# Stick-breaking attention on one core: one mask product for the two diagonal blocks of a PSUM bank, masks between a block's two products, and the shorter block first

## The chip, the cores and the metric

The kernel runs on one core of one Trainium2 chip. The metric is the device time of one execution in microseconds; of the kernel before, three executions gave 873.54, 874.85 and 875.4 us, with a median of 874.85 us. A separate execution was profiled, and every time below that is not one of these three comes from it.

## What is computed

The program is a whole decoder block for 512 tokens of width 1024: an RMS norm, one wide input projection, stick-breaking attention and an RWKV-7 branch beside each other, a merge with gates, an MLP, a gated per-layer embedding and a last norm. The change lies in the attention, whose reference for one block of 128 queries is

```python
z = jnp.einsum('bhqd,bhkd->bhqk', q[:, :, q0:kend], k[:, :, :kend]).astype(jnp.float32) * scale
mask = s_pos < t_pos
log_om = jnp.where(mask, jax.nn.log_sigmoid(-z), 0.0)
rev = lax.cumsum(log_om, axis=log_om.ndim - 1, reverse=True)
log_w = jax.nn.log_sigmoid(z) + rev - log_om
w = jnp.where(mask, jnp.exp(log_w), 0.0)
outs.append(jnp.einsum('bhqk,bhkd->bhqd', w.astype(v.dtype), v[:, :, :kend]))
```

There are 8 heads of width 64, and a key counts only for later queries, so on the diagonal block of each key block the mask is a triangle.

## The kernel before

Keys lie on partitions and queries on columns. For one head the scores are four key blocks j = 0 to 3 of 128 keys each; block j holds the queries from j\*128 on, so the blocks are 512, 384, 256 and 128 columns wide. They fill three PSUM banks (2 KB per partition, 512 columns of float32): bank 0 holds block 0, bank 2 holds block 2, and bank 1 holds block 1 in its columns 0 to 383 and block 3 in its columns 384 to 511. `BLOCKS` (L431) gives the order of the banks and of the blocks inside one: bank 2, bank 1, bank 0.

`scores` (L440) makes one head's scores. For every block it issues three products on TensorE into the bank, `ps_z`: L453, the keys `kk` against the rounded queries `qq`; L454, the same keys against the remainders `ql`; and L455, an identity `ident_b` against the triangle `caus_b` of -1e30 and 0, both in bf16, which adds the mask to the first 128 columns of the block (its diagonal). When a bank has all its products, ScalarE takes Abs, Exp and Ln of it (L458 to L460), VectorE makes the softplus `sp` (L461), and `split` (L221, L222) turns that into a high and a low part, `sph` and `spl`. After bank 1, sums of softplus over later key blocks are made too (L465 to L476: `sums`, `sums_hi`, `sums_lo`).

`attend` (L479) goes over the banks in the same order. It adds to the same PSUM bank the running sums inside a key block (L500, weights `tri`) and those of the later key blocks (L504, weights `neg`), ScalarE takes the exponential (L505), VectorE makes its high and low parts `wh` and `wl` (L506, L507), and `output` (L488, its product L492) multiplies these with the values `vv` into `ps_o`.

Eight such heads run one after another. `drive` (L279) mixes three streams by their counts of steps: `attend` of one head, `scores` of the next, and the projections of the weight units that come later. A projection step is `mm3` (L186): three products of 512 columns (L191, L192, L193). So between the pieces of the attention TensorE always has 512-column products standing in its queue. The order written so is then changed a little by a scheduler that puts what is ready first; after that each engine runs its own queue in order and waits where an operand is missing. Weights of every product are loaded anew: the trace has one LDWEIGHTS (engine PEld) for each MATMUL.

`z(zt, j, lo, n)` (L433) gives the columns of block j inside its bank.

Of the kernel before, what the change touches and what calls it, by code (L numbers as in the profile page):

```python
# [18 lines left out]
P = 128  # L19
T = 512  # L20
# [65 lines left out]
def tile_block(ctx: ExitStack, tc: tile.TileContext, xT, xt, pT, wts, lora, cols_d, gfin_d, consts_d, out, dbg=None):  # L86
    nc = tc.nc
    act, dve, pool, pe, sync = nc.scalar, nc.vector, nc.gpsimd, nc.tensor, nc.sync
# [3 lines left out]
    def r32(ap):  # L92
        return ap.bitcast(F32)
# [126 lines left out]
    def split(hi, lo, src):  # L220
        act.copy(out=hi, in_=src)  # L221
        dve.tensor_tensor(out=lo, in0=src, in1=r32(hi), op=ALU.subtract)  # L222
# [49 lines left out]
    with ExitStack() as sA:  # L272
# [43 lines left out]
        with ExitStack() as s1:  # L316
# [3 lines left out]
            def ps_z():  # L320
                return ps1.tile([P, T], F32, name="ps_z", bufs=5)
# [52 lines left out]
            ident_b, caus_b = (p1.tile([P, P], BF16, name=n, bufs=1) for n in ("ident_b", "caus_b"))  # L374
# [53 lines left out]
                    yield from product_steps(ps, w, h)  # L428
                    projected(hp, i, ps)

            BLOCKS = ((2, (2,)), (1, (1, 3)), (0, (0,)))  # L431

            def z(zt, j, lo=0, n=None):  # L433

                b = 0 if j == 0 else (2 if j == 2 else 1)
                s = ZB[j] - BANKS[b][0] + lo
                n = ZN[j] - lo if n is None else n
                return zt[b][:, s:s + n]

            def scores(hp, hh, got):  # L440

                qq, ql, kk = heads[hp][:3]
                sp = p1.tile([P, 1280], F32, name="sp")
                sph = p1.tile([P, 1280], F32R, name="sph")
                spl = p1.tile([P, 1280], F32R, name="spl")
                zt = {}
                got.update(zt=zt, sp=sp, sph=sph, spl=spl)
                for b, js in BLOCKS:
                    zt[b] = ps_z()

                    for j in js:
                        s = slice(j * P, (j + 1) * P)
                        pe.matmul(z(zt, j), kk[hh][:, s], qq[hh][:, j * P:T], start=j < 3, stop=False, skip_group_check=True)  # L453
                        pe.matmul(z(zt, j), kk[hh][:, s], ql[hh][:, j * P:T], start=False, stop=False, skip_group_check=True)  # L454
                        pe.matmul(z(zt, j, 0, P), ident_b, caus_b, start=False, stop=True, skip_group_check=True)  # L455
                    s, n = BANKS[b]
                    e = sp[:, s:s + n]
                    act.activation(out=e, in_=zt[b][:, :n], func=AF.Abs)  # L458
                    act.activation(out=e, in_=e, func=AF.Exp, scale=-1.0)
                    act.activation(out=e, in_=e, func=AF.Ln, bias=1.0)  # L460
                    dve.scalar_tensor_tensor(out=e, in0=zt[b][:, :n], scalar=0.0, in1=e, op0=ALU.max, op1=ALU.add)  # L461
                    split(sph[:, s:s + n], spl[:, s:s + n], e)
                    if b == 1:

                        sums = p1.tile([P, 512], F32, name="sums", bufs=1)  # L465
                        hi, lo = (p1.tile([P, 640], F32R, name=name) for name in ("sums_hi", "sums_lo"))
                        for to, i in ((0, 2), (256, 1)):
                            for part, d in ((sph, hi), (spl, lo)):
                                pool.tensor_copy(out=d[:, to:to + P], in_=part[:, ZB[i]:ZB[i] + P])
                        dve.tensor_tensor(out=sums[:, 0:P], in0=sp[:, ZB[2] + P:ZB[2] + 2 * P], in1=sp[:, ZB[3]:ZB[3] + P], op=ALU.add)  # L470
                        split(hi[:, P:2 * P], lo[:, P:2 * P], sums[:, 0:P])
                        for c, other in ((0, sp[:, ZB[2]:ZB[2] + P]), (P, sums[:, 0:P])):
                            dve.tensor_tensor(out=sums[:, 256 + c:384 + c], in0=sp[:, ZB[1] + P + c:ZB[1] + 2 * P + c], in1=other, op=ALU.add)
                        pool.tensor_copy(out=hi[:, 384:640], in_=sums[:, 256:512])
                        pool.tensor_tensor(out=lo[:, 384:640], in0=sums[:, 256:512], in1=r32(hi[:, 384:640]), op=ALU.subtract)
                        got["later"] = hi, lo  # L476
                    yield

            def attend(hp, hh, got):  # L479

                vv, oo = heads[hp][3:]
                sl = HALVES[hh]
                zt, sp, sph, spl = (got[n] for n in ("zt", "sp", "sph", "spl"))
                wh = p1.tile([P, 1280], F32R, name="wh")
                wl = p1.tile([P, 1280], F32R, name="wl")
                ps_o = ps1.tile([P, T], F32, name="ps_o", bufs=1)

                def output(js):  # L488

                    for j in js:  # L490
                        for part in (wh, wl):
                            pe.matmul(ps_o[:, j * P:T], vv[:, j, hh, :, :].rearrange("p a d -> p (a d)"),  # L492
                                      part[:, ZB[j]:ZB[j] + ZN[j]], start=j == 2 and part is wh, stop=j == 0 and part is wl,
                                      skip_group_check=True)

                before = ()
                for b, js in BLOCKS:
                    s, n = BANKS[b]
                    for part in (sph, spl):
                        pe.matmul(zt[b][:, :n], tri, part[:, s:s + n], start=False, stop=False, skip_group_check=True)  # L500
                    j = js[0]
                    for part, later in zip((sph, spl), got["later"]):
                        after = (later[:, 256:640], later[:, 0:256], part[:, ZB[3]:ZB[3] + P])[j]
                        pe.matmul(z(zt, j, P), neg, after, start=False, stop=part is spl, skip_group_check=True)  # L504
                    state["exp"] = act.activation(out=sp[:, s:s + n], in_=zt[b][:, :n], func=AF.Exp)  # L505
                    dve.tensor_copy(out=wh[:, s:s + n], in_=sp[:, s:s + n])  # L506
                    dve.tensor_tensor(out=wl[:, s:s + n], in0=sp[:, s:s + n], in1=r32(wh[:, s:s + n]), op=ALU.subtract)  # L507
                    yield
                    output(before)
                    before = js  # L510
                yield
                output(before)
                act.copy(out=oo[sl], in_=ps_o[64:128])
                dve.tensor_tensor(out=oo[sl], in0=ps_o[0:64], in1=oo[sl], op=ALU.add)
                if hh == 1:
                    sync.dma_start(out=o_sb[:, hp, :], in_=oo)
# [43 lines left out]
            ahead = with_late(early())  # L560
            NSTEP = 11
            drive((3, scores(*heads_[0], parts[heads_[0]])), (NSTEP, islice(ahead, NSTEP)))
            for n, g in enumerate(heads_):
                todo = [(5, attend(*g, parts[g])), (NSTEP, islice(ahead, NSTEP))]
                if n + 1 < len(heads_):
                    todo.insert(1, (3, scores(*heads_[n + 1], parts[heads_[n + 1]])))
                drive(*todo)
# [4 lines left out]
        with ExitStack() as s2:  # L572
# [37 lines left out]
            for hp in range(HP):  # L610
                csl = slice(hp * P, (hp + 1) * P)
                for i, (name, got) in enumerate((("w0", cum_), ("a0", a_all))):
# [3 lines left out]
                    t = p2.tile([P, T], F32, name=name, bufs=HP)  # L616
# [492 lines left out]
    def kept(tt):  # L1109
        t = p4.tile([P, 512], F32, name="pl", tag="rk", bufs=4)  # L1110
        return t

    for half in range(2):
        for tt in (half * 2, half * 2 + 1):
            t = kept(tt)
# [250 lines left out]
```

## Time and profile before

| | |
|---|---|
| profiled execution, device time | 874.59 us |
| its span in the trace | 872.8 us (1.79 us lie around it) |
| three executions without profile | 873.54, 874.85, 875.4 us |
| TensorE (PE) busy | 853.0 us, 98% |
| weight loads (PEld) busy | 687.9 us, 79% |
| VectorE (DVE) busy | 676.7 us, 78% |
| ScalarE (ACT) busy | 449.3 us, 51% |
| GpSimd (POOL) busy | 78.7 us, 9% |
| mean granted clock of TensorE | 0.995 |
| the scores and masks (L453 to L455) | from 31.4 to 125.9 us of the span |

Products on TensorE overlap, and their ends are modelled in the profile, so the busy time says little of how long a product holds the engine. What does is the distance from the start of one to the start of the next; a stretch of starts that begins and ends at products of the same kind gives the time that the products in it took.

### The profile page before, as it was taken

Reading aid. Unit: us, or ns where it says so; the run is one execution under the profiler, and the core shown is the slowest. Engines: PE = TensorE matmul, PEld = TensorE weight load, DVE = VectorE, ACT = ScalarE, POOL = GpSimd, SP = SyncE. Lnnn points to the kernel's source line nnn. Section 1 sums busy time; section 2 is a strip of 40 time slices with the busy share of each in tenths; the row PEclk is TensorE's granted clock in tenths of the full one; section 3 lists DMA queues with packets and bytes.
Section 4 is the critical chain, followed back from the end, with each engine's and each line's share of the span. In section 5 each row is a group of like instructions: output and inputs, shape, how many; then the busy total and the mean of one; then the engine's idle time right before and its main releaser. Section 6 shows DMA issues by size and latency. Waiting matters only on the chain.

```text
span 872.8 us, 13418 instructions
## 1 busy us (share of the span) xinstructions
PE 853.0 (98%) x5182; PEld 687.9 (79%) x5182; DVE 676.7 (78%) x1230; ACT 449.3 (51%) x706; POOL 78.7 (9%) x136
## 2 busy tenths in 40 slices
PE   9999999999999999998999999999999999999995
PEld 6778787877777777776888888888888888888885
DVE  7899987896979888666834789858985987697666
ACT  7888887735345253524524465344434533453743
POOL 1432421003202021010000000000000000000000
PEclk9999999999999999999999999999999999999998
DMA  7212113131221225357735621531252044200422
GB/s 269 97 62 72 62 61 103 54 101 47 73 74 61 86 75 176 102 174 266 272 97 170 240 73 34 186 119 49 87 178 97 25 141 149 97 1 0 171 71 97
DMA packets 32272, 95.32 MB, mean 109 GB/s; under 512 B 3664, under 2 KB 3664, under 8 KB 32208
## 3 DMA queue, kind: packets, MB, share of 16 engines
q1 hardware_dynamic: 32208, 94.46, 32.4%
q8 instruction: 41, 0.67, 0.3%
q14 instruction: 23, 0.19, 0.1%
HBM read 83.96 MB, written 10.49 MB: 108 GB/s over the span
## 4 chain that ended last, share of the span: by engine, by line
PE 74%; DVE 13%; ACT 7%; DMA 3%; issue 2%; SPq 0%; ACTq 0%; DVEq 0%
PE ps_m L191 13%; PE ps_m L193 13%; PE ps_m L192 13%; PE ps_m L208 7%; PE ps_m L206 7%; PE ps_m L207 7%; DVE w_lo L176 2%; DMA w_raw<-in_wts_dram 1%; ACT hx L1039 1%; PE ps_o L492 1%; PE ps_g L898 1%; DVE LX L836 1%; PE ps_z L500 1%; PE ps_s L936 1%; PE ps_c L927 1%
## 5 line engine op out<-in xcount | busy, mean ns | idle before, releaser
L175 ACT CAST w_hi<-w_raw 128x1024 fp32r<-128x1024 f32 x94 | 99.0, 1053 | 175.6 <-PE ps_m L192 114.8
L176 DVE TENSOR_TENSOR w_lo<-w_raw,w_hi 128x1024 fp32r<-128x1024 f32 x94 | 115.2, 1225 | 38.2 <-ACT w_hi L175 37.7
L191 PE MATMUL ps_m<-h_hi,w_hi 128*128 128x512 f32 x320 | 130.7, 410 | 0.0
L192 PE MATMUL ps_m<-h_lo,w_hi 128*128 128x512 f32 x320 | 128.9, 403 | 0.0
L193 PE MATMUL ps_m<-h_hi,w_lo 128*128 128x512 f32 x320 | 127.6, 399 | 0.0
L191 PE MATMUL ps_m<-hx,w_hi 128*128 128x512 f32 x256 | 99.7, 390 | 0.4 <-ACT hx L1039 0.4
L192 PE MATMUL ps_m<-hx,w_hi 128*128 128x512 f32 x256 | 99.6, 390 | 0.0
L193 PE MATMUL ps_m<-hx,w_lo 128*128 128x512 f32 x256 | 99.5, 389 | 0.0
L193 PEld LDWEIGHTS ps_m<-h_hi,w_lo 128*128 128x128 f32 x320 | 60.3, 188 | 11.7
L192 PEld LDWEIGHTS ps_m<-h_lo,w_hi 128*128 128x128 f32 x320 | 60.5, 189 | 11.3 <-DVE h_lo L349 1.1
L191 PEld LDWEIGHTS ps_m<-h_hi,w_hi 128*128 128x128 f32 x320 | 60.7, 190 | 10.5 <-ACT h_hi L348 0.4
L191 PEld LDWEIGHTS ps_m<-hx,w_hi 128*128 128x128 f32 x256 | 48.0, 188 | 10.4 <-ACT hx L1039 0.6
L192 PEld LDWEIGHTS ps_m<-hx,w_hi 128*128 128x128 f32 x256 | 48.1, 188 | 10.2 <-DVE hx L1040 0.2
L193 PEld LDWEIGHTS ps_m<-hx,w_lo 128*128 128x128 f32 x256 | 48.1, 188 | 9.9
L206 PE MATMUL ps_m<-w_hi,fS 128*128 128x512 f32 x128 | 49.8, 389 | 0.0
L207 PE MATMUL ps_m<-w_lo,fS 128*128 128x512 f32 x128 | 49.8, 389 | 0.0
L208 PE MATMUL ps_m<-w_hi,fS 128*128 128x512 f32 x128 | 49.8, 389 | 0.0
L208 PE MATMUL ps_m<-w_hi,fA 128*128 128x512 f32 x96 | 37.3, 389 | 0.0
L206 PE MATMUL ps_m<-w_hi,fA 128*128 128x512 f32 x96 | 37.3, 389 | 0.0
L207 PE MATMUL ps_m<-w_lo,fA 128*128 128x512 f32 x96 | 37.3, 389 | 0.0
L221 ACT CAST fS<-sums 128x256 fp32r<-128x256 f32 (+1 forms) x32 | 19.9, 620 | 33.3 <-DVE sums L1131 33.3
L1204 DVE TENSOR_TENSOR xs<-ps_m,xs 128x512 f32<-128x512 f32 x56 | 35.8, 681 | 0.0
(378 smaller groups left out, 1876.0 us busy)
## 6 DMA issues: line engine op xcount, KB each, us to landing
w_raw<-in_wts_dram SPq DMA_DIRECT2D x98, 512.0 KB, 3.4
gates<-gg SPq DMA_DIRECT2D x16, 256.0 KB, 2.0
x_in<-in_xT_dram SPq DMA_DIRECT2D x8, 256.0 KB, 5.1
tmp<-gates SPq DMA_DIRECT2D x8, 256.0 KB, 4.2
upsb<-tmp SPq DMA_DIRECT2D x8, 256.0 KB, 2.8
ga<-upsb SPq DMA_DIRECT2D x8, 256.0 KB, 6.3
gb<-gates SPq DMA_DIRECT2D x8, 256.0 KB, 5.8
xs<-in_xt_dram SPq DMA_DIRECT2D x4, 512.0 KB, 7.8
```

The costliest lines, as they stand in the source:

```text
L175: act.copy(out=hi, in_=raw)
L176: dve.tensor_tensor(out=lo, in0=raw, in1=r32(hi), op=ALU.subtract)
L191: pe.matmul(ps, wh, xh[:, k, t], start=first, stop=False)
L192: pe.matmul(ps, wh, xl[:, k, t], start=False, stop=False)
L193: pe.matmul(ps, wl, xh[:, k, t], start=False, stop=last)
L206: pe.matmul(ps, xh[:, k + j], wh, start=first and j == 0, stop=False, skip_group_check=True)
L207: pe.matmul(ps, xh[:, k + j], wl, start=False, stop=False, skip_group_check=True)
L208: pe.matmul(ps, xl[:, k + j], wh, start=False, stop=last and j == 1, skip_group_check=True)
L221: act.copy(out=hi, in_=src)
L492: pe.matmul(ps_o[:, j * P:T], vv[:, j, hh, :, :].rearrange("p a d -> p (a d)"), part[:, ZB[j]:ZB[j] + ZN[j]], start=j == 2 and part is wh, ...
L500: pe.matmul(zt[b][:, :n], tri, part[:, s:s + n], start=False, stop=False, skip_group_check=True)
L1204: dve.tensor_tensor(out=xb, in0=pss[t2], in1=xb, op=ALU.add)
```

## The change

```diff
-            BLOCKS = ((2, (2,)), (1, (1, 3)), (0, (0,)))
+            BLOCKS = ((2, (2,)), (1, (3, 1)), (0, (0,)))
...
-                    for j in js:
+                    n = len(js)
+                    diagonal = zt[b].rearrange("p (q t) -> p q t", t=P)[:, 0::3, :] if n == 2 else z(zt, js[0], 0, P)
+                    mask = caus_b.rearrange("p (o t) -> p o t", o=1).broadcast_to([P, n, P]) if n == 2 else caus_b
+                    for i, j in enumerate(js):
                         s = slice(j * P, (j + 1) * P)
-                        pe.matmul(z(zt, j), kk[hh][:, s], qq[hh][:, j * P:T], start=j < 3, stop=False, skip_group_check=True)
-                        pe.matmul(z(zt, j), kk[hh][:, s], ql[hh][:, j * P:T], start=False, stop=False, skip_group_check=True)
-                        pe.matmul(z(zt, j, 0, P), ident_b, caus_b, start=False, stop=True, skip_group_check=True)
+                        pe.matmul(z(zt, j), kk[hh][:, s], qq[hh][:, j * P:T], start=i == 0, stop=False, skip_group_check=True)
+                        if i == n - 1:
+                            pe.matmul(diagonal, ident_b, mask, start=False, stop=False, skip_group_check=True)
+                        pe.matmul(z(zt, j), kk[hh][:, s], ql[hh][:, j * P:T], start=False, stop=True, skip_group_check=True)
...
-                    j = js[0]
+                    j = js[-1]
```

In bank 1 the two blocks change places, so the 128-column block 3 comes first, in `scores` and in `output`. Their two masks become one product of 256 columns: it reads the triangle twice and writes two runs of 128 columns, the first and the last quarter of the bank. And the mask of every bank now stands between the last block's product with `qq` and its product with `ql`, where it stood behind both. Per head there are 11 products in place of 12, and 88 in place of 96 in all.

On TensorE bank 1 of a head in the steady stretch (the third head, the products before it are the last of `attend` for the head ahead) reads before

```order
L504 MATMUL ps_z<-sums_lo,neg 128x384
L453 MATMUL ps_z<-qq_407,kk_524 128x384
L454 MATMUL ps_z<-ql_195,kk_524 128x384
L455 LDWEIGHTS ident_b
L455 MATMUL ps_z<-caus_b,ident_b 128x128
L453 MATMUL ps_z<-qq_407,kk_524 128x128
L454 MATMUL ps_z<-ql_195,kk_524 128x128
L455 LDWEIGHTS ident_b
L455 MATMUL ps_z<-caus_b,ident_b 128x128
L191 MATMUL ps_m<-h_hi,w_hi 128x512
```

and with the change (L457, L459 and L460 are its lines of the `qq`, mask and `ql` products, L509 is the old L504)

```order
L509 MATMUL ps_z<-sums_lo,neg 128x384
L457 MATMUL ps_z<-qq_406,kk_522 128x128
L460 MATMUL ps_z<-ql_195,kk_522 128x128
L457 MATMUL ps_z<-qq_406,kk_522 128x384
L459 LDWEIGHTS ident_b
L459 MATMUL ps_z<-caus_b,ident_b 128x2x128
L460 MATMUL ps_z<-ql_195,kk_522 128x384
L191 MATMUL ps_m<-h_hi,w_hi 128x512
```

One mask and one load of the identity are gone, and no product of 128 columns stands ahead of a weight load of the 512-column stream any more.

The only other place where operations changed their order among themselves is on VectorE and ScalarE while the second head's bank 1 is worked on, some 46 us into the span. VectorE's queue there reads before (L461 makes the softplus of bank 1, L506 and L507 the parts of the first head's bank 0)

```order
L461 SCALAR_TENSOR_TENSOR sp<-ps_z,sp 128x512
L470 TENSOR_TENSOR sums<-sp 128x128
L506 CAST wh<-sp 128x512
L473 TENSOR_TENSOR sums<-sp 128x128
L507 TENSOR_TENSOR wl<-sp,wh 128x512
L222 TENSOR_TENSOR spl<-sp,sph 128x512
L222 TENSOR_TENSOR sums_lo<-sums,sums_hi 128x128
L473 TENSOR_TENSOR sums<-sp,sums 128x128
```

and with the change (L466, L475, L478, L511 and L512 are the old L461, L470, L473, L506 and L507)

```order
L466 SCALAR_TENSOR_TENSOR sp<-ps_z,sp 128x512
L511 CAST wh<-sp 128x512
L475 TENSOR_TENSOR sums<-sp 128x128
L512 TENSOR_TENSOR wl<-sp,wh 128x512
L222 TENSOR_TENSOR spl<-sp,sph 128x512
L222 TENSOR_TENSOR sums_lo<-sums,sums_hi 128x128
L478 TENSOR_TENSOR sums<-sp 128x128
L478 TENSOR_TENSOR sums<-sp,sums 128x128
```

`wh` moves ahead of the first sum, and one sum moves behind `wl`. On ScalarE the Abs of the next bank 0 moves ahead of the small cast `sums_hi` at the same place. GpSimd's queue and SyncE's (which issues the DMAs) keep their order.

## The prediction

> **What bounds the kernel now.** I read the page first: span, busy shares, the chain that ended last.
>
> ```profile
> span 872.8 us, 13418 instructions
> PE 853.0 (98%) x5182; PEld 687.9 (79%) x5182; DVE 676.7 (78%) x1230; ACT 449.3 (51%) x706; POOL 78.7 (9%) x136
> ...
> PE 74%; DVE 13%; ACT 7%; DMA 3%; issue 2%; SPq 0%; ACTq 0%; DVEq 0%
> ```
>
> TensorE is the bound over most of the span, and the chain lies on it for 74%; for 13% it lies on VectorE. So a change on TensorE counts where TensorE's own queue sets the pace, and not where it stands waiting for VectorE. Then I read TensorE's timeline at bank 1 of the fourth head, a stretch where it never waits. Columns: start, duration, engine, line, operation.
>
> ```profile
> 68.48 0.33 PE L453 MATMUL ps_z<-qq,kk 128*128 128x384 f32 x1
> 68.65 0.34 PE L454 MATMUL ps_z<-ql,kk 128*128 128x384 f32 x1
> 68.83 0.23 PE L455 MATMUL ps_z<-caus_b,ident_b 128*128 128x128 bf16 x1
> 68.87 0.31 PE L453 MATMUL ps_z<-qq,kk 128*128 128x128 f32 x1
> 69.02 0.27 PE L454 MATMUL ps_z<-ql,kk 128*128 128x128 f32 x1
> 69.13 0.23 PE L455 MATMUL ps_z<-caus_b,ident_b 128*128 128x128 bf16 x1
> 69.17 0.48 PE L191 MATMUL ps_m<-h_hi,w_hi 128*128 128x512 f32 x1
> 69.48 0.39 PE L192 MATMUL ps_m<-h_lo,w_hi 128*128 128x512 f32 x1
> 69.72 0.39 PE L193 MATMUL ps_m<-h_hi,w_lo 128*128 128x512 f32 x1
> ```
>
> Starts, not durations, tell what a product costs. The 384-column product takes 0.17 us to the next start (68.48 to 68.65), so a 512-column one in proportion 0.23 (69.48 to 69.72 shows 0.24, with the rounding). From 68.48 to 69.48 are 1.00 us; less 0.23 for the 512-column product at its end, bank 1 costs **0.77 us**. Its columns alone (two of 384 for 0.17 each, and four of 128 for some 0.06 each, a quarter of 0.23) would cost 0.58. The missing 0.19 sit behind the products of 128 columns. The cause shows in the next stretch, two 128-column products between 512-column ones:
>
> ```profile
> 71.67 0.22 PE L492 MATMUL ps_o<-wh,vv 128*128 128x128 f32 x1
> 71.73 0.27 PE L492 MATMUL ps_o<-wl,vv 128*128 128x128 f32 x1
> 71.84 0.45 PE L191 MATMUL ps_m<-h_hi,w_hi 128*128 128x512 f32 x1
> 72.13 0.40 PE L192 MATMUL ps_m<-h_lo,w_hi 128*128 128x512 f32 x1
> ```
>
> From 71.67 to 72.13 are 0.46; less 0.23, two such products cost 0.23, or **0.115 each** and not 0.06. That is what two 256-column products cost as well, so 0.115 us is a floor per product, set by the weight load that comes behind it. Bank 2 shows that row, and what one mask costs alone:
>
> ```profile
> 63.98 0.28 PE L453 MATMUL ps_z<-qq,kk 128*128 128x256 f32 x1
> 64.10 0.28 PE L454 MATMUL ps_z<-ql,kk 128*128 128x256 f32 x1
> 64.22 0.23 PE L455 MATMUL ps_z<-caus_b,ident_b 128*128 128x128 bf16 x1
> 64.26 0.47 PE L191 MATMUL ps_m<-h_hi,w_hi 128*128 128x512 f32 x1
> 64.57 0.39 PE L192 MATMUL ps_m<-h_lo,w_hi 128*128 128x512 f32 x1
> ```
>
> 256 columns take 0.12 (63.98 to 64.10). The mask takes 64.22 to 64.57 less 0.23, or **0.12**, twice its columns' 0.06. The loads themselves:
>
> ```profile
> L453 PEld LDWEIGHTS ps_z<-qq,kk 128*128 128x128 f32 x32 | 6.1, 192 | 1.4 <-issue 0.8
> L455 PEld LDWEIGHTS <-ident_b 128*128 128x128 bf16 x32 | 3.1, 96 | 3.8 <-issue 3.5
> ```
>
> A float32 load is recorded with 192 ns and the identity's in bf16 with 96 ns. From 68.83 to 69.48 are 0.65, less 0.23 are 0.42: two masks of 0.12 and one short product of 0.115 leave 0.06 for the short product ahead of the identity. So the floor holds ahead of a float32 load, and ahead of the identity only the columns count.
>
> **The change part by part.** *Bank 1.* After it: two 128-column products ahead of float32 loads, 0.23 together; the 384-column `qq` product 0.17; the 256-column mask; the 384-column `ql` product 0.17. No row has the mask's new form (two runs written, one triangle read twice). From below it is 0.115, the floor. From above I take the slowest narrow product of the trace, in plain float32:
>
> ```profile
> 285.46 0.93 PE L832 MATMUL ps_g<-tmp,cst 128*128 128x392 f32 x2 [0.41 <-DVE tmp L828]
> 285.93 0.70 PE L192 MATMUL ps_m<-h_lo,w_hi 128*128 128x512 f32 x1
> ```
>
> 392 columns hold TensorE 0.47 us, so 256 columns at that rate 0.31. The nearest row is the contiguous 256-column product with 0.12, and that I take: 0.23 + 0.17 + 0.12 + 0.17 = 0.69, against 0.77. Bank 1 saves **0.08 us** a head, or 8 x 0.08 = 0.6 us for eight heads, if all passes on. With the mask at 0.31 it would lose 0.11 a head.
>
> [...]
>
> *Banks 2 and 0.* The mask moves ahead of the `ql` product. Behind it there stands a float32 load either way (of `kk` now, of `w_hi` before), so it costs 0.12 both times: nothing on TensorE. The bounds are 0.06 a bank either way, all that a load leaves uncovered, or 16 x 0.06 = 1.0 us; I take nothing, since the 0.12 was read where the same kind of load follows. But the bank's last product now ends 0.06 us later, since the uncovered load comes inside the bank. Abs waits for it, which costs only where ScalarE is next to starving, in the first head:
>
> ```profile
> 32.14 0.38 ACT L458 ACTIVATE sp<-ps_z 128x256 f32<-128x256 f32 x1
> 32.55 0.42 ACT L459 ACTIVATE sp<-sp 128x256 f32<-128x256 f32 x1
> 32.87 0.58 ACT L458 ACTIVATE sp<-ps_z 128x512 f32<-128x512 f32 x1
> ```
>
> There ScalarE has work without a gap from bank to bank, so 0.06 to 0.1 us are what the delay can cost; later heads' banks stand ready long before.
>
> *Output.* Blocks 3 and 1 change places in L492: the same four products, two of them short, both ahead of float32 loads before and after. Nothing.
>
> *What passes on.* Of eight heads, the first two end in waits for VectorE. The second head's place is the one with the changed order:
>
> ```profile
> 46.72 0.29 DVE L470 TENSOR_TENSOR sums<-sp 128x128 f32<-128x128 f32 x1
> 46.93 0.42 DVE L506 CAST wh<-sp 128x512 fp32r<-128x512 f32 x1
> 47.26 0.28 DVE L473 TENSOR_TENSOR sums<-sp 128x128 f32<-128x128 f32 x1
> 47.46 0.78 DVE L507 TENSOR_TENSOR wl<-sp,wh 128x512 fp32r<-128x512 f32 x1
> ```
>
> ```profile
> 46.89 0.40 PE L193 MATMUL ps_m<-h_hi,w_lo 128*128 128x512 f32 x1
> 47.40 0.50 PE L492 MATMUL ps_o<-wh,vv 128*128 128x512 f32 x1
> ...
> 48.29 0.50 PE L492 MATMUL ps_o<-wl,vv 128*128 128x512 f32 x1 [0.16 <-DVE wl L507]
> ```
>
> TensorE waits here, first for `wh`, then for `wl`. With one sum (0.20 us from start to start, 47.26 to 47.46) behind `wl`, both come some 0.2 us earlier, and TensorE resumes at 48.1 in place of 48.29. The sum that is put off is needed only by L504 of the next head's attend, some microseconds later; that wait does not appear. What the first two heads save in bank 1 is swallowed by this wait, and the second head may bring its softplus 0.05 later, since its 384-column pair now stands behind the wait for `spl` and not ahead of it. So this place gives 0.2 less 0.05 less 0.06: **0.1 us**.
>
> The fifth head's bank 1 lies ahead of a stretch in which VectorE is the bound, and its saving is lost there:
>
> ```profile
> 80.00:95.00 15.00, 14.16 (x74) 11.34 (x73) 14.23 (x24) 12.81 (x24) 6.29 (x8) 1.00 0.27 88
> ```
>
> ```profile
> 92.83 0.39 PE L193 MATMUL ps_m<-h_hi,w_lo 128*128 128x512 f32 x1
> 93.51 0.38 PE L492 MATMUL ps_o<-wh,vv 128*128 128x256 f32 x1 [0.30 <-DVE wh L506]
> 94.44 0.39 PE L492 MATMUL ps_o<-wl,vv 128*128 128x256 f32 x1 [0.54 <-DVE wl L507]
> ```
>
> VectorE (the third busy time of the row, after PE and PEld) is busy 14.23 of 15 us, and TensorE stands still twice at its end. Heads 3, 4, 6, 7 and 8 remain, 5 x 0.08 = **0.4 us**. From the end of the attention on, each queue has the order that it had, so I let the lead pass to the end of the program.
>
> *The sum.* 0.4 + 0.1 = 0.5 us off TensorE's pace; some of it I expect to end in the short waits of the RWKV stage, and take 0.4. From the profiled execution, 872.8 + 1.79 = 874.59 us, that is **874.2 us**. The profiled execution stands 0.26 us under the median of the three runs, which themselves spread from 873.54 to 875.4; the change is smaller than that spread.
>
> [...]
>
> **The rivals.** *All is absorbed.* The lead is 0.4 us, and TensorE waits for VectorE in several places after the attention; if VectorE sets the pace at one of them by work that the lead does not touch, the time is 874.6. For it speaks VectorE's 13% of the chain; against it that VectorE's work there hangs on products of TensorE.
>
> *The mask in two runs is slow.* This ends slower than before. At 0.31 us a mask eight heads lose 8 x (0.31 - 0.12) = 1.5 us against the forecast, **875.7 us**. It decides from 0.17 us on, where 8 x 0.05 = 0.4 eats the gain, and passes 0.2% (1.75 us) only above 0.39 us a mask, (1.75 + 0.4) / 8 over 0.12; the 0.47 of the L832 row would make 877.0. Against it: the columns in a run are adjacent, and the same triangle is read at full speed today. [...]
>
> *A wait further on changes its size.* The longest single wait of TensorE is
>
> ```profile
> PE ps_c L979 <- DVE y L974: 2.9, 1, 2.9
> ```
>
> If a shift of some tenths lets another operation in ahead of it, it can vanish or come twice: 871.3 or 877.1. With the same order in each queue I see no reason for it.
>
> **How the numbers follow.** The forecast, 874.0 to 874.4, has 0.55; absorbed 0.18; the slow mask 0.15, of which 0.05 above 0.39 us; a later wait 0.12, half each way. The range leaves out the later waits and the dearest masks, 0.17 together: 872.7 to 876.2. It holds the mask's bounds (0.115 and 0.31 us, 874.2 and 875.7) and the moved masks' (873.2 and 875.2), and beside them half a microsecond for the spread of the runs. About 0.2% is what a measurement of this kernel can tell from no change: faster than that 0.06 (the wait gone), within it 0.83, slower 0.11 (the wait twice, the dearest masks).
>
> **What would show it.** In the profile of the changed kernel: bank 1 of the fourth head, from its first product to the second 512-column product behind it, at 0.92 in place of 1.00; the 256-column mask followed by its `ql` product with 0.12 in all; TensorE's second L492 row near 48 us some 0.1 to 0.2 earlier; the wait before 94.4 a little longer, and its end tied to VectorE. A mask of 0.2 us or more, or a new wait after the attention, makes the prediction wrong.

## The result, and the profile after

The changed kernel takes **876.48 us** (median of 20 runs, 874.28 to 880.38), the kernel before 873.67 us beside it (20 runs, 871.83 to 876.09). The ratio is 1.0031, with a 95% interval of 1.0022 to 1.0041: **slower by 0.31%**, some 2.8 us. I had forecast 874.2 us, with no difference that can be measured. Four lines of the page of the changed kernel, to be held against those of before: the span, the busy shares, the instruction queue of the DMA engines (packets, MB, share) and the chain.

```profile
span 875.0 us, 13403 instructions
...
PE 851.6 (97%) x5174; PEld 687.0 (79%) x5174; DVE 676.7 (77%) x1230; ACT 449.1 (51%) x706; POOL 78.9 (9%) x136
...
q8 instruction: 41, 0.67, 0.3%
...
PE 72%; DVE 14%; ACT 7%; DMA 4%; issue 2%; SPq 0%; ACTq 0%; DVEq 0%
```

TensorE is busy 1.4 us less, as it should be with a product less per head, and yet the span is 2.2 us longer. So the loss is no work; it is time in which TensorE stands still or runs slowly. First the place of the change, bank 1 of the fourth head, from TensorE's timeline after:

```profile
68.50 0.22 PE L457 MATMUL ps_z<-qq,kk 128*128 128x128 f32 x1
68.56 0.27 PE L460 MATMUL ps_z<-ql,kk 128*128 128x128 f32 x1
68.67 0.39 PE L457 MATMUL ps_z<-qq,kk 128*128 128x384 f32 x1
68.90 0.28 PE L459 MATMUL ps_z<-caus_b,ident_b 128*128 128x256 bf16 x1
68.94 0.42 PE L460 MATMUL ps_z<-ql,kk 128*128 128x384 f32 x1
69.20 0.40 PE L191 MATMUL ps_m<-h_hi,w_hi 128*128 128x512 f32 x1
69.43 0.39 PE L192 MATMUL ps_m<-h_lo,w_hi 128*128 128x512 f32 x1
```

From the first start to the second 512-column product are 69.43 less 68.50, or 0.93 us, against 1.00 before. Within one head the change does what was forecast. To find where the rest went, I set TensorE's starts of both profiled executions side by side, row by row. The distance (after less before) is -0.30 us at 126, +0.06 at 297.8, +2.12 at 300.5, +3.21 at 307.4, +2.49 at 407.6, +0.90 at 410.7, and it stays at +0.91 to TensorE's last product; the outputs come 2.2 us later. The first large step is one stop, in a burst of 64 small products. TensorE's timeline after, with the idle time and its releaser in brackets:

```profile
297.80 0.87 PE L817 MATMUL ps_g<-LX,LB 32*32 32x64 f32 x47
300.51 0.46 PE L817 MATMUL ps_g<-LX,LB 32*32 32x64 f32 x17 [1.85 <-issue]
300.90 0.72 PE L192 MATMUL ps_m<-h_lo,w_hi 128*128 128x512 f32 x1
```

and before (L812 is the old L817):

```profile
297.74 1.10 PE L812 MATMUL ps_g<-LX,LB 32*32 32x64 f32 x64
298.76 0.50 PE L192 MATMUL ps_m<-h_lo,w_hi 128*128 128x512 f32 x1
```

Before, the 64 products run as one group. After, 47 of them run, and the 48th starts 2.06 us behind the 47th. No operand is missing: the bracket says "issue", time in which the engine waited for nothing that the profile shows, and the stop lies inside a group whose operands all came before its first product. The stop is 160 us behind the last product of the attention (137.7). Behind it stands a second loss, in the profile after by stretches of 1 us; the column behind the busy times is TensorE's granted clock:

```profile
300.00:301.00 1.00, 0.49 (x18) 0.40 (x18) 0.00 (x0) 0.00 (x0) 0.00 (x0) 1.00 0.00 0
301.00:302.00 1.00, 1.00 (x3) 0.81 (x4) 0.99 (x3) 0.34 (x1) 0.00 (x0) 0.51 0.06 16
302.00:303.00 1.00, 1.00 (x4) 0.52 (x2) 0.96 (x2) 1.00 (x2) 0.00 (x0) 0.50 0.00 0
303.00:304.00 1.00, 1.00 (x56) 0.74 (x59) 0.00 (x0) 0.24 (x1) 0.00 (x0) 0.50 0.18 70
304.00:305.00 1.00, 1.00 (x31) 0.75 (x19) 0.59 (x2) 0.00 (x0) 0.00 (x0) 0.79 0.51 193
```

From 301.0 to 304.4 TensorE gets half its clock: 3.4 us that hold 1.7 us of work. Of these 1.7, only 1.1 show in the distance (2.12 to 3.21), since not all of that stretch hangs on TensorE. The kernel before has such a stretch as well, at another place, behind its longest wait for VectorE (from 406.4 to 409.8):

```profile
407.00:408.00 1.00, 1.00 (x4) 0.81 (x3) 0.90 (x2) 0.00 (x0) 0.00 (x0) 0.50 0.48 82
408.00:409.00 1.00, 1.00 (x3) 0.71 (x3) 0.32 (x2) 0.62 (x1) 0.00 (x0) 0.50 0.83 254
```

In this execution the changed kernel has none there, which gives 1.6 us back (2.49 to 0.90). That is why only 0.9 us of 3.2 reach TensorE's end in this pair of profiles, while the medians lie 2.8 us apart.

The last loss comes at the end of the program, where ScalarE waits for the last weight units (`wg`, by the line that rounds them). After:

```profile
834.93 1.05 ACT L175 CAST wg<-w_raw 128x1024 fp32r<-128x1024 f32 x1 [1.65 <-DMA w_raw<-in_wts_dram]
839.34 1.05 ACT L175 CAST wg<-w_raw 128x1024 fp32r<-128x1024 f32 x1 [3.36 <-DMA w_raw<-in_wts_dram]
```

Before:

```profile
834.12 1.05 ACT L175 CAST wg<-w_raw 128x1024 fp32r<-128x1024 f32 x1 [1.74 <-DMA w_raw<-in_wts_dram]
837.13 1.05 ACT L175 CAST wg<-w_raw 128x1024 fp32r<-128x1024 f32 x1 [1.96 <-DMA w_raw<-in_wts_dram]
```

The last unit's wait grew from 1.96 to 3.36 us. With the 0.9 us of TensorE this makes the 2.2 us of the end: ScalarE and VectorE carry the delay of that unit to the outputs.

### The profile page after: what moved, and what is told of

Same layout as the page of the kernel before. It is cut to its first block, busy times and chain, and to the rows that moved or that the text cites. A ratio compares the mean times of both kernels' runs of the same rounds, so it can differ in the third digit from the quotient of the medians.

```text
span 875.0 us, 13403 instructions
## 1 busy us (share of the span) xinstructions
PE 851.6 (97%) x5174; PEld 687.0 (79%) x5174; DVE 676.7 (77%) x1230; ACT 449.1 (51%) x706; POOL 78.9 (9%) x136
## 4 chain that ended last, share of the span: by engine, by line
PE 72%; DVE 14%; ACT 7%; DMA 4%; issue 2%; SPq 0%; ACTq 0%; DVEq 0%
PE ps_m L191 13%; PE ps_m L193 13%; PE ps_m L192 13%; PE ps_m L208 7%; PE ps_m L207 7%; PE ps_m L206 7%; DVE w_lo L176 2%; DMA w_raw<-in_wts_dram 1%; ACT hx L1044 1%; PE ps_g L817 1%; PE ps_o L497 1%; PE ps_g L903 1%; DVE LX L841 1%; ACT w_hi L175 1%; PE ps_s L941 1%
## 5 line engine op out<-in xcount | busy, mean ns | idle before, releaser
L191 PE MATMUL ps_m<-h_hi,w_hi 128*128 128x512 f32 x320 | 128.2, 402 | 0.6 <-ACT h_hi L348 0.6
L192 PEld LDWEIGHTS ps_m<-hx,w_hi 128*128 128x128 f32 x256 | 48.1, 188 | 10.2 <-DVE hx L1045 0.2
L193 PEld LDWEIGHTS ps_m<-hx,w_lo 128*128 128x128 f32 x256 | 48.1, 188 | 9.8
```

Of the source, the lines that this page charges most:

```text
L191: pe.matmul(ps, wh, xh[:, k, t], start=first, stop=False)
L192: pe.matmul(ps, wh, xl[:, k, t], start=False, stop=False)
L193: pe.matmul(ps, wl, xh[:, k, t], start=False, stop=last)
```

## The experiments

**The theories.** A: the operations of the change are not slow at all. The change has 8 matmuls and 8 weight loads fewer, and so moves the places at which TensorE's instructions are fetched from memory; one fetch now comes too late in a burst in which TensorE uses its instructions up quickly (64 products and their loads in 1.10 us), and another lies beside the last weight transfer. The profile speaks for it with its q8 row. 41 packets of 0.67 MB in all are 16 KB each, and TensorE's 2 x 5182 instructions before, divided by 41, are some 250 a packet. The packets' times in the trace of before give 256: from the start of the first packet to that of the last TensorE starts 10246 instructions, semaphore instructions with them, and divided by 40 that is 256.15. The rival: the new operations or their order in the attention cause it, by a slower mask, or by what they shift on VectorE. All runs of a group were compared with runs of the kernel before on the same chip, 17 to 33 of them.

**The merge alone.** From the kernel before, in the old order of blocks (`diagonal` and `mask` are made as in the change):

```diff
...
                     for j in js:
...
-                        pe.matmul(z(zt, j, 0, P), ident_b, caus_b, start=False, stop=True, skip_group_check=True)
+                    pe.matmul(diagonal, ident_b, mask, start=False, stop=True, skip_group_check=True)
```

> One part alone: the two masks of bank 1 as one product of 256 columns, at the bank's end; blocks in the old order, the other masks at their old places. TensorE's program is 16 instructions shorter (8 products and 8 weight loads), as in the changed kernel. Theory A (the shorter program moves TensorE's instruction fetches, and one of them is missed inside the burst of small products near 298 us): a stop of some 2 us at that burst, and a time 1.5 to 3 us above the kernel before, though the attention itself gets no slower. Theory B (the order of the masks and blocks costs, by later Abs or shifted waits): no slower than before, 0 to 0.5 us under it.

Measured: 876.56 us, a ratio of 1.0025 (1.0008 to 1.0041). The stop is there, in TensorE's timeline:

```profile
298.16 0.87 PE L815 MATMUL ps_g<-LX,LB 32*32 32x64 f32 x47
300.97 0.46 PE L815 MATMUL ps_g<-LX,LB 32*32 32x64 f32 x17 [1.94 <-issue]
```

and so is the half clock (301.9 to 305.4) and a last weight wait of 3.57 us. The merge alone brings the whole loss, with the same 47 and 17.

**The places alone.** Short block first and each mask between its block's two products, but two masks, so the count of instructions is that of before:

```diff
-            BLOCKS = ((2, (2,)), (1, (1, 3)), (0, (0,)))
+            BLOCKS = ((2, (2,)), (1, (3, 1)), (0, (0,)))
...
-                        pe.matmul(z(zt, j), kk[hh][:, s], ql[hh][:, j * P:T], start=False, stop=False, skip_group_check=True)
-                        pe.matmul(z(zt, j, 0, P), ident_b, caus_b, start=False, stop=True, skip_group_check=True)
+                        pe.matmul(z(zt, j, 0, P), ident_b, caus_b, start=False, stop=False, skip_group_check=True)
+                        pe.matmul(z(zt, j), kk[hh][:, s], ql[hh][:, j * P:T], start=False, stop=True, skip_group_check=True)
...
```

> The other part alone: the short block first and every mask between a block's two products, but two masks of 128 columns in bank 1, so TensorE's program is as long as before. Theory A: no stop at the burst near 298 us, and a time within 0.5 us of the kernel before. Theory B: 1.5 to 3 us above it.

Measured: 873.63 us, 0.9992 (0.9982 to 1.0002), and the 64 products in one group. The order makes no difference that can be measured. It still leaves the rival a way: the merged mask itself could be what delays. That is decided by leaving the change whole and giving back the places.

**The change with 16 instructions more ahead of it.** The warm-up at the start of the program, 12 products of 512 columns, becomes 20 products with the same number of columns:

```diff
-            for _ in range(12):
-                pe.matmul(ps, warm[:, 0:P], warm, start=True, stop=True)
+            for n in [512] * 4 + [256] * 16:
+                pe.matmul(ps[:, 0:n], warm[:, 0:P], warm[:, 0:n], start=True, stop=True)
```

> The changed kernel whole, with its 12 products for warming up (512 columns each, at the very start, nobody reads them) cut into 4 of 512 and 16 of 256 columns: as many columns, and 16 instructions more, so that from there on TensorE's program stands where it stood before the change. Theory A: the stop near 298 us is gone, and the time is 0 to 0.6 us under the kernel before. Theory B and the theory that the wide mask is slow: it stays 1.5 to 3 us above.

Measured: 872.77 us, 0.9985 (0.9973 to 0.9997). The burst is whole again, its start earlier than that of before (297.74):

```profile
297.50 1.10 PE L817 MATMUL ps_g<-LX,LB 32*32 32x64 f32 x64
```

No half clock follows it, and the last weight wait is 1.81 us. All of the loss has gone with eight more products in the warm-up, whose results nothing uses. Theory A stands, the rival falls.

**Other counts.** The same line with `[384] * 4 + [192] * 24` (32 instructions more):

> As the run before, with 28 products for warming up (4 of 384 and 24 of 192 columns, again as many columns): 32 instructions more than the changed kernel, 16 more than before the change. Theory A: the fetch falls at another place again; whether a stop comes can't be said beforehand, but if one comes it is inside a burst of small products and has a fetch of 16 KB beside it. Theory B: 1.5 to 3 us above the kernel before.

Measured: **870.88 us**, 0.9959 (0.9945 to 0.9973), the fastest of all. No stop, last weight wait 1.89, and the long wait for VectorE near 402 is shorter too (1.84 us from start to start, 3.25 before). With `[512] * 8 + [256] * 8` (8 more):

> The changed kernel with 8 products for warming up of 512 and 8 of 256 columns: 8 instructions more than the changed kernel, 8 fewer than before the change. Theory A in the form that the fetch is missed because it is asked for just behind a weight transfer of 512 KB that is issued near 295.3 us: it is asked for some 0.9 us earlier, goes ahead of the transfer, and the stop near 298 us is gone, though the edge of the block still lies inside the burst of small products; time within 0.2% of the kernel before. Theory D (an edge inside the burst is enough): the stop stays, four products earlier in the burst, and the time is 1.5 to 3 us above the kernel before.

Measured: 875.98 us, 1.0029 (1.0013 to 1.0045), with the stop and the half clock. Half the way back is not enough: where the fetch was expected in time with eight instructions back, that was wrong. The stop only moved from the 47th product to the 43rd:

```profile
297.86 0.85 PE L817 MATMUL ps_g<-LX,LB 32*32 32x64 f32 x43
300.66 0.53 PE L817 MATMUL ps_g<-LX,LB 32*32 32x64 f32 x21 [1.95 <-issue]
```

Four products earlier are eight instructions (a load and a matmul each), which is the size of the padding: the stop sits at one place in the row of instructions, by my reading the end of what had been fetched, and not at an operation. With `[256] * 24` (24 more):

> The changed kernel with 24 products for warming up of 256 columns each: 24 instructions more than the changed kernel, 8 more than before the change. Theory A: no stop near 298 us, and a time between those with 16 and with 32 more, 0.15 to 0.4% under the kernel before. Theory B: 1.5 to 3 us above it.

Measured: 871.41 us, 0.9969 (0.9957 to 0.9981), no stop. One weight unit near the end waits 3.02 us here, but the next one only 0.66.

**The kernel before with 16 instructions more**, by the same edit:

> The kernel before, with nothing of the change, and its 12 products for warming up cut into 4 of 512 and 16 of 256 columns: 16 instructions more, so TensorE's program stands where it stands in the changed kernel with 32 more. Theory A (the places of the instruction fetches make the differences): 0.2 to 0.4% faster than the kernel before, some 0.5 us above the changed kernel with 32 more. Theory C (that kernel's gain is the change's own, set free): within 0.1% of the kernel before.

Measured: 871.83 us, 0.9979 (0.9968 to 0.999). The kernel before, too, had places that could be bettered: its long wait near 402 and its half clock behind it are gone or short (1.43 us from start to start).

**Sixteen instructions late.** The places are given back only behind the burst, by eight extra 128-column products in the MLP (0.9 us of useless work):

```diff
+            for _ in range(8 if (qd, m) == (2, 0) else 0):
+                pe.matmul(ps[:, 0:P], w[0][:, 0:P], hx[0][:, 0, 0:P], start=True, stop=True)
```

> The changed kernel with 8 more products of 128 columns in the MLP (third quarter, first unit; the real product that follows overwrites them, and they cost TensorE 8 x 0.115 = 0.9 us): what lies ahead keeps the changed kernel's places, what lies behind has the places of before. Theory A: the stop near 298 us stays, and the last weight unit near 835 us no longer comes late (ScalarE's wait for it 2.0 us in place of 3.4); time 0.9 - 1.3 = 0.4 us under the changed kernel, 1 to 2.5 us above the one before. If the late unit has another cause: the wait stays at 3.4, and the time is 0.9 us above the changed kernel.

Measured: 876.56 us, 1.0034 (1.002 to 1.0047). The stop stays (2.25 us from start to start), and the last weight wait is back at 1.79 us:

```profile
837.06 1.05 ACT L175 CAST wg<-w_raw 128x1024 fp32r<-128x1024 f32 x1 [1.79 <-DMA w_raw<-in_wts_dram]
```

So the two losses come apart: the stop stays with the count ahead of 298, and the weight wait changes with the count ahead of its own place. The count alone does not set that wait, though: the places alone, with the count of before, has 2.81 us there, and the change + 8 has 2.52; by the packets (below) it goes with where the fetch falls beside the transfer. The time did not fall by 0.4 us, as was expected with the second loss gone: the 0.9 us of useless work and the scatter of the half clocks hide what it is worth, so this run shows the wait, not its price.

**Why the fetch is late.** In the trace, the packets of the instruction queue have times. These are the one ahead of the burst and the weight or gate transfer that ended just before it, worked out from the packets (not a view of the profile):

```
kernel                      instructions   transfer         fetch starts   stop
                            ahead (to before)
before                       0             290.83-292.96    293.22         none
change + 16                  0             290.58-292.91    293.11         none
places alone                 0             291.82-294.11    294.09         none
change                     -16             296.25-298.49    298.31         2.06
merge alone                -16             296.60-298.78    298.67         2.15
change + 8                  -8             296.29-298.41    298.33         2.17
```

In each kernel the fetch starts as a transfer of 512 KB ends, and in the three with the stop it is the next weight unit's. So it could be late because it stands behind that transfer. The test cuts this one transfer from 512 KB to 64 KB; GpSimd zeroes the rest of the buffer, so that one unit of the weights is left out in large part.

```diff
-                sync.dma_start(out=loaded[i], in_=unit(i))
+                sync.dma_start(out=loaded[i][:, 0:1024 if i != 37 else 128], in_=unit(i)[:, 0:1024 if i != 37 else 128])
+                if i == 37:
+                    pool.memset(loaded[i][:, 128:1024], 0.0)
```

> The changed kernel with one weight transfer cut: of the unit that SyncE issues at 295.30 us only 128 of 1024 columns are loaded (64 KB for 512 KB), and GpSimd fills the rest of its buffer with zeros, so that unit's product is not the reference's; every queue keeps its order. Theory B (TensorE's instruction fetch stands behind this weight transfer in the DMA engines): with the transfer gone after some 0.3 us the fetch starts before 297.5 and not at 298.3, TensorE does not stop inside the burst of 64 small products, or stops under 0.5 us, and the time falls by 2 to 3.7 us against the changed kernel, to 0.999 to 1.001 of the kernel before. Theory D (the fetch is asked for late because of the count of instructions alone, whatever else the DMA engines carry): the fetch starts at 298.0 to 298.7 as in the three kernels with 16 or 8 instructions fewer, the stop of 2.0 to 2.3 us stays, and the time stays at 1.002 to 1.004 of the kernel before. Both: bank 1 as in the changed kernel.

Measured: 875.39 us, 1.0018 (1.0005 to 1.003), 1.1 us under the changed kernel (876.48, in another group of runs). It lies between the two expectations, and the intervals of the two ratios overlap, so the time alone decides nothing; the profile says more. The DMA engines' share of each microsecond (the column ahead of GB/s) in the changed kernel

```profile
296.00:297.00 1.00, 1.00 (x74) 0.93 (x75) 0.54 (x3) 0.00 (x0) 0.00 (x0) 1.00 0.53 127
297.00:298.00 1.00, 1.00 (x44) 0.93 (x44) 0.70 (x2) 0.10 (x1) 0.00 (x0) 1.00 0.94 373
```

and with the short transfer

```profile
296.00:297.00 1.00, 1.00 (x77) 0.96 (x78) 0.54 (x3) 0.00 (x0) 0.10 (x1) 1.00 0.31 82
297.00:298.00 1.00, 1.00 (x48) 0.93 (x47) 0.62 (x2) 0.18 (x1) 0.00 (x0) 1.00 0.00 0
```

The transfer now ends at 296.71, the fetch starts at 296.74 in place of 298.31, and the stop is half as long, 1.09 us from start to start:

```profile
297.72 0.86 PE L819 MATMUL ps_g<-LX,LB 32*32 32x64 f32 x47
299.45 0.46 PE L819 MATMUL ps_g<-LX,LB 32*32 32x64 f32 x17 [0.87 <-issue]
```

In both kernels TensorE goes on 1.3 to 1.4 us after the fetch's packet has ended (299.24 to 300.51, 298.08 to 299.45). So about half the stop is the fetch standing behind the weight transfer. For the other half, the fetch starts 3.5 us later than in the kernel before (296.74 against 293.22) even with the transfer out of its way. No run tested what makes it so late: 16 instructions are eight products, some 1.8 us of the 512-column stream (8 x 0.23), and that alone would have put it at about 295, where the DMA engines were idle (a share of 0.00 from 295 to 296 in the changed kernel). Behind the shorter stop no half clock followed at 301.

The traces say something of it. Number TensorE's instructions (products, loads, semaphore instructions) in the order of their starts. Of the 574 fetches in the 14 traces none starts before the 150th instruction past a multiple of 256, and 132 start at about the 153rd; the others start later. In the changed kernel the 153rd for the fetch ahead of the burst begins at 294.6. Ten instructions on stands one that waits, the first load of an earlier burst, for VectorE:

```profile
296.03 0.64 PEld L817 LDWEIGHTS ps_g<-LX,own 32*32 32x32 f32 x64 [0.35 <-DVE own L848]
```

This load is the 163rd in the four kernels with 16 instructions fewer and the 171st in the change + 8, all with the stop; in every kernel without the stop it is the 179th or a later one. With no transfer near, a fetch elsewhere comes about 1 us behind such a wait: in the kernel before, products that waited until 313.88 and 336.57 (the 171st and the 175th) have a fetch at 314.99 and 337.55, and in the changed kernel one that waited until 341.04 (the 165th) has it at 342.07. With the short transfer the load starts at 295.95 and the fetch at 296.74. So it reads as if TensorE asks for its next packet too late because it stands at that load, and the change moved the place of the asking from ahead of the load to behind it; with the whole transfer the fetch then also finds the DMA engines taken.

**More instructions, or better places?** To tell these apart, the kernel before gets the 32 instructions of the fastest version, the fastest version is run again beside it, and the change gets 48 (`[256] * 12 + [128] * 24`), so that its places are those of the kernel before with 32.

> The kernel before with a warm-up of 4 products of 384 and 24 of 192 columns for 12 of 512 (the same columns, 32 TensorE instructions more). Theory A (the places of the fetches make the difference, and the gain of the padded changed kernel is a better set of places plus the 0.5 us of the change itself): no stop near 298, and a time 0.1% to 0.4% under the kernel before, 0.05% to 0.2% over the padded changed kernel of this call if its places are as good. Rival (the padded changed kernel is faster by the change and the padding does nothing for the kernel before): within 0.1% of the kernel before.

Measured: 876.56 us, 1.0017 (1.0004 to 1.0029). This was expected by neither: more instructions made the kernel before slower. No stop at 298, but the last weights come late again:

```profile
832.03 1.05 ACT L175 CAST wg<-w_raw 128x1024 fp32r<-128x1024 f32 x1 [3.56 <-DMA w_raw<-in_wts_dram]
833.25 1.05 ACT L175 CAST wg<-w_raw 128x1024 fp32r<-128x1024 f32 x1 [0.17 <-DMA w_raw<-in_wts_dram]
837.73 1.05 ACT L175 CAST wg<-w_raw 128x1024 fp32r<-128x1024 f32 x1 [3.42 <-DMA w_raw<-in_wts_dram]
```

> The changed kernel with 32 TensorE instructions more in the warm-up, a second time, beside the kernel before with the same warm-up. Theory A: no stop near 298, 0.995 to 0.997 of the kernel before, as the first time (0.9959). Rival (its first result was luck of one chip): 0.998 or more.

Measured: 870.6 us, 0.996 (0.9945 to 0.9974), as the first time.

> The changed kernel with a warm-up of 12 products of 256 and 24 of 128 columns for 12 of 512 (the same columns, 48 TensorE instructions more), so that behind the attention its instructions stand where those of the kernel before with 32 more stand, which is 0.17% over the kernel before. Theory A (the places set the stops; the change by itself is worth 0.15% to 0.2%): 0.998 to 1.001 of the kernel before, slower than with 32 more (0.996), no stop near 298, the waits for the last weights longer than 3 us again. Rival (a longer warm-up, or more instructions, by itself makes the changed kernel faster): 0.995 to 0.997, as with 32 more.

Measured: 874.59 us, 1.0004 (0.999 to 1.0018), with the late weights of the kernel whose places it shares:

```profile
831.83 1.05 ACT L175 CAST wg<-w_raw 128x1024 fp32r<-128x1024 f32 x1 [3.53 <-DMA w_raw<-in_wts_dram]
833.10 1.06 ACT L175 CAST wg<-w_raw 128x1024 fp32r<-128x1024 f32 x1 [0.22 <-DMA w_raw<-in_wts_dram]
837.59 1.05 ACT L175 CAST wg<-w_raw 128x1024 fp32r<-128x1024 f32 x1 [3.44 <-DMA w_raw<-in_wts_dram]
```

So it is the places and not the number. These waits, too, have a fetch beside them: in the kernel before with 32 more one starts at 829.8, 2.5 us after the weight unit's issue at 827.3, and in the change with 48 more at 828.7, 1.8 us after the issue at 826.9, both inside the unit's transfer. In the changed kernel one starts at 835.5, 0.9 us after the issue at 834.6. From issue to the rounding these units take 4.7 to 4.9 us, others 3.4 to 3.5 (834.6 to 839.34 in the changed kernel, against 833.7 to 837.13 in the kernel before, whose fetch starts at 833.4, ahead of the issue). The packets show how: in the changed kernel the fetch lasts from 835.45 to 837.18, and the last seven packets of the unit end one by one, some 0.16 us apart, from 837.97 to 838.91, where in the kernel before the last twelve end together within 0.4 us (836.38 to 836.77). That a fetch delays a transfer is read from these times and was not tested by itself.

**The change at equal places.** Three pairs have the same count ahead of every later instruction: change + 16 and before, 0.9985; change + 32 and before + 16, 0.9959 / 0.9979 = 0.998; change + 48 and before + 32, 1.0004 / 1.0017 = 0.9987. At equal places the change is so 0.13% to 0.2% faster, some 1.1 to 1.7 us; only the first pair was measured side by side with its own interval (0.9973 to 0.9997), and the intervals behind the third quotient do not keep it clear of no difference. This is more than the 0.5 us that the sum gave the change, and it holds half clocks too: in the first pair's profiles TensorE is 0.2 us ahead at 400 and 2.2 us ahead at 410, behind the half clock of the kernel before, which the change + 16 has not.

## Why the prediction was wrong, step by step

**Bank 1, right.** Forecast 0.69 us in place of 0.77; measured 0.93 less 0.23, or 0.70. Only the sum can be compared, since by starts the two short products take 0.17, the mask 0.04 and its `ql` product 0.26; it came out as worked out from the contiguous rows. The upper end of the forecast, 874.4 us, stands for a smaller saving in this bank, with a time of a short product that no run shows: the rows of before have 0.115 us for it, and after the bank saves 0.07 (1.00 to 0.93).

**The mask in two runs, right.** From the mask's start to the second 512-column product are 0.53 us (68.90 to 69.43); less the 0.17 of the `ql` product and 0.23 of the 512-column one, 0.13 are left, against 0.12 forecast for contiguous columns. A slower product by its two runs does not show here, at least for runs of 128 adjacent columns. The rival that was built on it named 875.7 us, near the result, and had nothing to do with it. Its bound of 0.31 us came from a row of two products (x2), which start at 285.46 and 285.90; with the 512-column product behind them they take until 286.70, so some 0.50 us each and not 0.47, and nothing hangs on it here.

**The fifth head, right.** Its saving ends in a longer wait, as forecast; it is the wait for `wh` that grew, though, from 0.30 to 0.45 us:

```profile
93.43 0.38 PE L497 MATMUL ps_o<-wh,vv 128*128 128x256 f32 x1 [0.45 <-DVE wh L511]
94.36 0.38 PE L497 MATMUL ps_o<-wl,vv 128*128 128x256 f32 x1 [0.55 <-DVE wl L512]
```

**The place near 48 us, undecided.** The product that waits for `wl` starts at 48.40 and not at 48.1. But this execution came to the attention 0.6 us later than that of before (29.82 against 29.22 at the same product), by its start; the wait swallows that difference too.

**What passes on, right up to 126 us.** Behind the wait near 48 us the distance goes from +0.09 us at 50 to -0.30 at 126, or 0.39, against 0.4 in the sum for the heads 3, 4, 6, 7 and 8; in the change + 16 it goes from -0.12 to -0.46, or 0.34.

**The step that failed** is "From the end of the attention on, each queue has the order that it had, so I let the lead pass to the end of the program." The queues have their order, but not their places: 16 instructions fewer on TensorE put each later fetch of instructions at another moment. What it cost, by the profiled pair: 2.1 us for the stop at 298, 1.1 for the half clock behind it and 1.3 for the last weights, less the 0.7 that later waits gave back (3.21 to 2.49) and less the 1.6 us of before's own half clock. The sum held no term for any of them. The lead itself also did not reach that far, for the reason that the rival of absorption gave: at 148 TensorE waits for `lxl` of VectorE, and 0.25 us of lead (at 140) is gone, where the sum had taken off 0.1 (before, the product starts at 148.60):

```profile
148.69 0.47 PE L620 MATMUL ps_g<-lxl,lw 128*128 128x512 f32 x1 [0.25 <-DVE lxl L613]
```

**The rival of a later wait** named the right kind of event, a size of 2.9 us and both signs, but tied it to another operation that goes in ahead, and gave it 0.12 for "I see no reason for it". It also looked only at waits that the profile of before shows; the stop at 298 is none of them. The range ended at 876.2, 0.3 us under the result, because the dear half of this rival (877.1) was left out.

## What to carry to other kernels

A change that takes instructions away from a long straight program moves every later instruction fetch, and with a gain of some tenths of a per cent this can decide the sign, as it did here: look in the profile after for "issue" stops inside a group of small products, far from the change, before blaming the changed lines. The control is cheap: give the missing instructions back where they do no work, and compare both kernels at equal places. Here that showed a change 0.13% to 0.2% faster at equal places behind a measured loss of 0.31%, and a warm-up of 28 short products in place of 12 long ones took the changed kernel to 0.996 of the kernel before.

## What the runs showed of the hardware

Four to 24 products more in the warm-up, at the same number of columns, moved the time by several us, in either direction: over six counts for the change (0, 8, 16, 24, 32 and 48 instructions more) the ratio went 1.0031, 1.0029, 0.9985, 0.9969, 0.9959, 1.0004, and for the kernel before (0, 16, 32) 1, 0.9979, 1.0017.

TensorE's instructions come in packets of 16 KB, and in the six kernels of the table above each fetch ahead of the burst started within 0.3 us of the end of a data transfer; cutting that transfer to an eighth brought the fetch 1.6 us forward and halved the stop. No fetch of the 14 traces starts before the 150th instruction past a multiple of 256.

The clock went to half after a stop of 2.06 to 2.17 us in three profiles (the change, the merge alone, the change + 8), but not after 2.25 us (the sixteen late, where products of 512 columns behind the stop start 0.23 us apart) nor after 1.09 (the short transfer, with a granted clock of 1.00 from 300 to 304). In the changed kernel the half clock lasted 3.41 us (301.01 to 304.43), and as long in the kernel before (406.39 to 409.80), there behind the wait for VectorE of 2.87 us. The stops of the three profiles have small products on both sides. What starts a half clock in one execution and not in another is not shown. The times of the changed kernel's 20 runs rise as their mean granted clock falls: 874.28 to 875.44 us at 0.996 to 0.997, 875.94 to 877.24 at 0.994 to 0.995, 878.01 to 880.38 at 0.991 to 0.993. By estimate, one stretch of half clock more lowers that mean by 0.002 (1.7 of 875 us), so the groups would fit with one such stretch between each and the next. No run tested that.
